# First tiles turned on TensorE, weights fetched ahead, and rows of tokens four tiles ahead, in a hybrid decoder step

## The chip, the core and the metric

The kernel runs on one core of one Trainium2 chip. The metric is the device time of one execution in microseconds (us), the median of several runs. The names of the engines: PE is TensorE (its weight loads are PEld), DVE is VectorE, ACT is ScalarE, POOL is GpSimd, SP is SyncE, which here issues all DMAs. An engine works through its instructions in a fixed order; where one of them waits, those behind it wait too.

## What is computed

One layer of a decoder with two kinds of mixers, for a prompt of 2048 tokens and for 64 sample tokens (8 sequences of 8). The rows x of 1024 numbers are normed, multiplied by one weight matrix of 3600 columns, and the columns are split up:

```python
def mixer_layer(x, pos, attend, s0, norm_w, w_in, ...):
    h = rmsnorm(x, norm_w)
    z = h @ w_in
    q, k, v, qb, kb, vb, g_lr, gate_a, gate_b = jnp.split(z, split_points(), axis=-1)
    q = rope(rmsnorm(heads(q, H_A), q_norm_w), pos)
    k = rope(rmsnorm(heads(k, H_A), k_norm_w), pos)
    o_a = attend(q, k, v)
    ...
    o_b, s_fin = gla_chunked(...)
    mixed = concatenate([o_a * silu(gate_a), rmsnorm(o_b) * silu(gate_b)])
    return x + mixed @ w_out, k, v, s_fin
```

`attend` is a mixture of three dilated windows over 8 heads of 64; `gla_chunked` is gated linear attention with 4 heads. Everything is in float32.

## The kernel before

**Products.** A product of float32 accuracy is made from float16 parts. A value is scaled and split into a high part (its float16) and a low part (the rest, as float16); three products (high by high, high by low, low by high) are summed in PSUM. For each row tile of 128 tokens and each block of weights (`v`, `q`, `k`, `qkb`, `g`, `vb`, `gb`, most with 512 columns) that is 8 slices of the contraction by 3 products, 24 matmuls at L1056. The 64 sample rows hold both parts in one stationary operand, 16 matmuls at L769.

**A row tile** (`prep`, L474): the row comes by DMA (`fetch`, L464), ACT squares and sums it (L487), `rsqrt` (L118) makes the scale with a few small steps on DVE and two on ACT, ACT writes the high part (L495), DVE the low part (L496). A DMA transpose turns both (L499) into `hl`, one of four buffers, the stationary operand; `hl` is also stored to DRAM for the later blocks (L503). The first four rows have two double buffers (tag `qq`) and a room of their own for the parts (`early_ht`); from tile 4 on there is one buffer for a row (tag `x`) and one for its parts (`ht`). The sample's rows are turned by PE (L510).

**A block of weights** (`load_w`, L544): eight DMAs bring 128x512 raw weights into eight buffers (tag `wr`). Then comes a size for the scale: for `v` the exact largest absolute value, by eight reductions on DVE (L566); for all other blocks a sum of squares, by eight steps on ACT (L572). `spread_max` (L533) takes the largest over the partitions by way of PE (L536, L539) and DVE (L538). From it a power of two follows, and then ACT writes the eight high parts (L603) and DVE the eight low parts (L604).

**The order of work.** First come `v`'s weights, the sample's rows and tiles 0 to 3 (L955 to L959). `first(0)` (L1076) then multiplies v for the sample and tiles 0 to 3, then q, then k. q's weights are loaded and split behind v's tile 0, k's behind v's tile 3; behind k of tile t, row t+4 is fetched and prepared. `first(1)` to `first(3)` go tile by tile through v, q, k, while units of attention (`attend`, L395: scores L408, mask and maximum on DVE L416, exponential on ACT L419, turning L426, values L441) are worked through in between; behind tile t, row t+4 is fetched and prepared, up to tile 15. Each block's result has a post: v is scaled and stored (L726, L734, L735); q and k are copied (`zs`, one buffer, L640 and L648), squared (L647), summed (L649), rotated on POOL (L672, L678) and scaled on DVE (L683, L684), split and stored (L756 to L760). Behind that follow the rest of the attention with `qkb`, the linear attention with `g`, `vb` and `gb`, and the output projection (L1422). Constants (`tabs`, `m3w`, `gnw`) are loaded by SP after the first tiles' code.

The order of the instructions on each engine, DMA issues on SP among them, is set by a scheduler that plays the program through in a timeline of its own (`schedule_with_timeline_sim=True`) and puts first what is ready first there; the order of the code is a preference only.

Of the kernel before, what the change touches and what calls it, by code (L numbers as in the profile page):

```python
# [7 lines left out]
F32 = mybir.dt.float32  # L8
# [44 lines left out]
def tile_hymba(ctx: ExitStack, tc: tile.TileContext, A: dict):  # L53
# [56 lines left out]
    for r0 in (0, 64):  # L110
        DVE.tensor_copy(ident64[r0 : r0 + 64], ident8[r0 : r0 + 64, r0 : r0 + 64])
    ones = cp.tile([P, 1], F32, name="ones")
# [234 lines left out]
    with ExitStack() as c1:  # L347
# [13 lines left out]
        wr = right(c_in, "wr", 8)  # L361
# [17 lines left out]
        again = [0]  # L379

# [83 lines left out]
        def fetch(t):  # L464
            n = NS if t == "s" else P
            if t in (0, 1, 2, 3):
                if t % 2 == 0:
                    early.append(ap_.tile([P, 2, D], F32, name=f"x_{t}", tag="qq"))
                x = xs[t] = early[-1][:, t % 2]
            else:  # L470
                x = xs[t] = xp.tile([P, D], F32, name=f"x_{t}", tag="x", bufs=1)
            SP.dma_start(x[:n], x_s if t == "s" else x_p[t * P : (t + 1) * P, :])

        def prep(t):  # L474
            again[0] += 1
            n = NS if t == "s" else P
            u = again[0]
            x = xs.pop(t)[:]
            if t == "s":
                hs = hps.tile([P, KT, 2 * NS], F16, name="hs")  # L480
                hi, lo = hs[:, :, 0:NS], hs[:, :, NS:]
            else:
                hl = hp.tile([P, 2, KT, n], F16, name=f"hl_{u}", tag="hl")
                hi, lo = hl[:, 0], hl[:, 1]
            ss = sm.tile([P, 1], F32, name=f"ss_{u}", tag="ss")
            jk = zp.tile([P, D], BF16, name=f"jk_{u}", tag="z1")
            ACT.activation(jk[:n], x[:n], AF.Square, accum_out=ss[:n])  # L487
            rs = sm.tile([P, 1], F32, name=f"rs_{u}", tag="rs")
            rsqrt(sm, rs[:n], ss[:n], 1.0 / D, n, 1, f"x{u}", H_SCALE)
            if t != "s":  # L490
                if t < 4:
                    ht = early_ht[:, t]
                else:
                    ht = xp.tile([P, 2, D], F16, name=f"ht_{u}", tag="ht", bufs=1)[:]
                ACT.activation(ht[:, 0], x, AF.Copy, scale=rs[:])  # L495
                DVE.scalar_tensor_tensor(  # L496
                    ht[:, 1], x, rs[:], ht[:, 0], ALU.mult, ALU.subtract
                )
                SP.dma_start_transpose(  # L499
                    hl[:].rearrange("p a k c -> p (a k) c"), ht.rearrange("p a c -> p (a c)")  # L500
                )
                hT[t] = (hi, lo)
                SP.dma_start(h_d[t * P : (t + 1) * P, :], hl[:].rearrange("p a k c -> p (a k c)"))  # L503
                return
            DVE.tensor_scalar(x[:n], x[:n], rs[:n], None, ALU.mult)
            for half in range(2):
                pt = ps_P.tile([P, 512], F32, name=f"ptx_{u}_{half}", tag="PT")
                for i in range(4):
                    k = 4 * half + i
                    PE.transpose(  # L510
                        pt[:, i * n : (i + 1) * n], x[:n, k * P : (k + 1) * P], ident[:n, :n]
                    )
                ptv = pt[:, : 4 * n].rearrange("p (k c) -> p k c", k=4)
                h = hi[:, 4 * half : 4 * half + 4, :]
                ACT.activation(h, ptv, AF.Copy)
                DVE.tensor_tensor(
                    lo[:, 4 * half : 4 * half + 4, :], ptv, h, ALU.subtract
                )
            hT[t] = hs
# [24 lines left out]
        def load_w(name, between=(), behind=()):  # L544

            if name in ("o0", "o1"):
                src, c0, n, rows, sh = w_out, 512 * int(name[1]), 512, None, 1.0
            else:
                src, (c0, n), rows, sh = w_in, BLOCKS[name], nw, H_SCALE
            raws = []  # L550
            mx = sm.tile([P, KT], F32, name=f"wm_{name}", tag="wm")
            for k in range(KT):
                raw = wr.tile([P, 528], F32, name=f"wr_{name}_{k}", tag="wr")
                SP.dma_start(raw[:, :n], src[k * P : (k + 1) * P, c0 : c0 + n])
                raws.append(raw)
# [3 lines left out]
            for f in behind:  # L559
                fetch(f)  # L560


            exact = name == "v"
            for k in range(KT):
                if exact:
                    DVE.tensor_reduce(  # L566
                        mx[:, k : k + 1], raws[k][:, :n], AX.X, ALU.max, apply_absolute_value=True
                    )
                else:
# [3 lines left out]
                        jk[:, :n], raws[k][:, :n], AF.Square, accum_out=mx[:, k : k + 1], **by  # L573
# [27 lines left out]
            for k in range(KT):  # L601
                h, l = w[:, 0, k, :n], w[:, 1, k, :n]
                ACT.activation(h, raws[k][:, :n], AF.Copy, scale=nws[:, k : k + 1])  # L603
                DVE.scalar_tensor_tensor(  # L604
                    l, raws[k][:, :n], nws[:, k : k + 1], h, ALU.mult, ALU.subtract
# [1216 lines left out]
```

## Time and profile before

| what | value |
|---|---|
| median of 3 runs | 1446.03 us (1445.89 to 1446.85) |
| the profiled execution's own time | 1444.89 us |
| its span in the profile | 1443.1 us |
| busy: PE, DVE, ACT, POOL | 89%, 70%, 59%, 43% of the span |
| mean granted PE clock | 0.961 |
| chain that ended last, by engine | PE 35%, DVE 22%, DMA 19%, ACT 10%, issue 8%, POOL 4% |
| DMA, mean | 198 GB/s |

The span runs from the first to the last instruction; all times in the views are counted from its start. The chain that ended last is followed back from the last instruction, at each step to what released it. "Issue" is time in which an engine waited for nothing that the profile shows. `a<-b` means that a is written from b, by the program's names, without buffer numbers. Below, "landing" is the time from a DMA's issue to its arrival.

### The profile page before, as it was taken

Reading aid. Unit: us, or ns where it says so; the run is one execution under the profiler, and the core shown is the slowest. Engines: PE = TensorE matmul, PEld = TensorE weight load, DVE = VectorE, ACT = ScalarE, POOL = GpSimd, SP = SyncE. Lnnn points to the kernel's source line nnn. Section 1 sums busy time; section 2 is a strip of 40 time slices with the busy share of each in tenths; the row PEclk is TensorE's granted clock in tenths of the full one; section 3 lists DMA queues with packets and bytes.
Section 4 is the critical chain, followed back from the end, with each engine's and each line's share of the span. In section 5 each row is a group of like instructions: output and inputs, shape, how many; then the busy total and the mean of one; then the engine's idle time right before and its main releaser. Section 6 shows DMA issues by size and latency. Waiting matters only on the chain.

```text
span 1443.1 us, 26500 instructions
## 1 busy us (share of the span) xinstructions
PE 1287.7 (89%) x8878; PEld 741.6 (51%) x8878; DVE 1013.1 (70%) x2445; ACT 853.1 (59%) x2295; POOL 624.8 (43%) x564
## 2 busy tenths in 40 slices
PE   4797998998989799997799999989889979999997
PEld 1343554555546455565466755667545435444343
DVE  6486877888798967667765446899978698773222
ACT  6635677677558866767667764778777543221120
POOL 0052334466667545664420376655752364340000
PEclk9998998999999999999799999999999999999998
DMA  9857585477866798879876453343225769988661
GB/s 280 253 163 181 149 215 145 125 204 224 207 181 190 171 271 260 281 231 245 233 186 161 137 169 103 101 133 119 71 103 192 258 203 339 377 286 267 227 205 62
DMA packets 255194, 285.36 MB, mean 198 GB/s; under 512 B 126209, under 2 KB 157010, under 8 KB 255058
## 3 DMA queue, kind: packets, MB, share of 16 engines
q1 hardware_dynamic: 255058, 283.67, 67.0%
q8 instruction: 70, 1.15, 0.3%
q14 instruction: 66, 0.54, 0.1%
HBM read 183.19 MB, written 75.24 MB: 179 GB/s over the span
## 4 chain that ended last, share of the span: by engine, by line
PE 35%; DVE 22%; DMA 19%; ACT 10%; issue 8%; POOL 4%; SPq 2%; DVEq 0%; POOLq 0%; ACTq 0%
PE Y L1422 8%; DMA T_q<-qp_d 3%; PE acc_vb L1056 3%; PE acc_g L1056 3%; PE OS L1671 3%; DMA x<-in_x_prompt 2%; PE s L408 2%; PE acc_q L1056 2%; PE acc_qkb L1056 2%; DVE p L416 2%; PE acc_v L1056 2%; DVE qbd L221 2%; PE t L426 2%; PE acc_k L1056 2%; ACT p L419 2%
## 5 line engine op out<-in xcount | busy, mean ns | idle before, releaser
L925 POOL TENSOR_TENSOR pr<-k,qb 128x512 f32<-128x512 f32 x128 | 174.8, 1366 | 188.7 <-DVE sck L926 111.7
L1056 PEld LDWEIGHTS <-hr 128*128 128x128 f16 x1824 | 177.6, 100 | 137.7 <-issue 16.5
L419 ACT ACTIVATE p<-p,o 128x256 f32<-128x256 f32 (+1 forms) x384 | 173.2, 453 | 84.3 <-DVE o L416 72.5
L1056 PEld LDWEIGHTS <-hl 128*128 128x128 f16 x1248 | 124.9, 102 | 157.5 <-issue 39.4
L1422 PE MATMUL Y<-w_o,mh 128*128 128x512 f16 x768 | 183.6, 387 | 10.4 <-ACT mh L1388 6.0
L416 DVE CUSTOM_DVE_ANT_0 p<-s,m3w,scl_s 128x256 f32<-128x256 f32 (+1 forms) x384 | 143.4, 418 | 34.4 <-DMA o_d<-o 20.8
L393 POOL TENSOR_TENSOR pt<-p,pt 128x512 f16<-128x512 f32 (+1 forms) x80 | 92.9, 1162 | 139.6 <-ACT pt L392 90.5
L441 PE MATMUL O<-v,pt 128*128 128x128 f16 x1200 | 115.6, 223 | 27.0 <-POOL pt L393 11.4
L426 PE MATMUL t<-ident,p 128*128 128x128 f32 x600 | 117.8, 286 | 14.3 <-ACT p L419 13.2
L1422 PEld LDWEIGHTS <-mh 128*128 128x128 f16 x768 | 72.8, 99 | 106.2 <-issue 27.1
L926 DVE TENSOR_REDUCE sck<-pr 128x8 f32<-128x512 f32 x128 | 87.1, 680 | 56.3 <-POOL pr L925 55.8
L408 PE MATMUL s<-kk,qq 128*128 128x256 f16 (+1 forms) x512 | 107.6, 324 | 17.5 <-DVE o L416 12.6
L1056 PE MATMUL acc_v<-w_v,hl 128*128 128x512 f16 x384 | 101.1, 410 | 13.0 <-ACT zs_k L648 4.6
L441 PEld LDWEIGHTS <-pt 128*128 128x128 f16 x1200 | 85.6, 100 | 51.8 <-POOL pt L393 15.7
L1056 PE MATMUL acc_g<-w_g,hr 128*128 128x272 f16 (+1 forms) x768 | 105.6, 288 | 5.3 <-DVE za L775 3.9
L1056 PE MATMUL acc_q<-w_q,hl 128*128 128x512 f16 x384 | 96.2, 394 | 2.1 <-ACT zs_q L648 1.4
L1056 PE MATMUL acc_k<-w_k,hl 128*128 128x512 f16 x384 | 92.9, 385 | 2.7 <-ACT zs_k L648 2.7
L1388 ACT ACTIVATE mh<-tm 128x1024 f16<-128x1024 f16 x32 | 31.7, 1020 | 104.1 <-PE tm L1387 97.7
L1056 PE MATMUL acc_vb<-w_vb,hr 128*128 128x512 f16 x384 | 91.4, 381 | 1.9 <-DVE so_g L622 1.9
L426 PEld LDWEIGHTS t<-ident,p 128*128 128x128 f32 x600 | 72.0, 145 | 36.0 <-ACT p L419 23.7
L1056 PE MATMUL acc_gb<-w_gb,hr 128*128 128x512 f16 x384 | 88.6, 384 | 0.1
L210 ACT ACTIVATE E<-D_e 128x256 f32<-128x256 f32 (+1 forms) x168 | 67.6, 412 | 31.7 <-DVE ks L217 21.2
(527 smaller groups left out, 2640.2 us busy)
## 6 DMA issues: line engine op xcount, KB each, us to landing
k<-in_cache_k_win SPq DMA_DIRECT2D x104, 256.0 KB, 4.4
sv<-in_cache_v_win SPq DMA_DIRECT2D x104, 256.0 KB, 5.5
hr<-h_d SPq DMA_DIRECT2D x44, 512.0 KB, 4.5
qb<-q_d SPq DMA_DIRECT2D x64, 256.0 KB, 4.7
oc<-o_d SPq DMA_DIRECT2D x48, 264.0 KB, 5.7
o_d<-o SPq DMA_DIRECT2D x64, 132.0 KB, 3.4
x<-in_x_prompt SPq DMA_DIRECT2D x16, 512.0 KB, 5.2
h_d<-hl SPq DMA_DIRECT2D x16, 512.0 KB, 5.1
```

The lines of the kernel that those rows point to most:

```text
L210: ACT.activation(E[rows, i, :n], D[rows, half], AF.Exp, scale=1.0 / 16.0)
L393: POOL.tensor_tensor(l, f, h, ALU.subtract)
L408: PE.matmul(s_ps[:, i * w : (i + 1) * w], q, k, start=(n == 0), stop=(n == len(prods) - 1),)
L416: DVE.tensor_tensor_reduce(s[:, sl], s_ps[:, sl], mask, neg, BIG, ALU.add, ALU.min, nmf(i))
L419: ACT.activation(s[:, sl], s[:, sl], AF.Exp, bias=nmf(i), scale=-1.0, accum_out=denf(i))
L426: PE.transpose(p_ps[:, i * P : (i + 1) * P], t["s"][:, i * P : (i + 1) * P], ident[:])
L441: PE.matmul(o_, t["pt"][:, c, (i * nb + b) * P : (i * nb + b + 1) * P], vf(i, b), start=(n == 0), stop=(n == 2 * nb - 1),)
L925: POOL.tensor_tensor(pr[:], kt, qt, ALU.mult)
L926: DVE.tensor_reduce(out, pr[:].rearrange("p (u k d) -> p u k d", u=2, k=4), AX.X, ALU.add)
L1056: PE.matmul(z, a_[:, k, :], w[:, p_, k, cols], start=(k == 0 and i == 0), stop=(k == KT - 1 and i == 2),)
L1422: PE.matmul(Y[:], a_[:, k, :], w_[:, part, k, :512], start=(i == 0), stop=(i == len(prods) - 1),)
L1671: PE.matmul(OS[32 * x : 32 * x + 32, 0:256], ps(x), vs_[bb][:, 256 * u : 256 * u + 256], start=(i == 0), stop=(i == 13),)
```

## The change

It touches the beginning of the kernel, up to the last prepared tile:

- Tiles 0 to 3 are turned by PE (64 transposes of 128x128 float16 with a float16 identity) into PSUM; ACT copies out the high parts, DVE the low parts. From tile 4 on, the DMA transpose stays.
- The order of ACT's instructions in this part is written out (`manual_schedule`): squares of the sample and tile 0, then tile 1's squares ahead of tile 0's scaling, the sample's copies, tile 0's copy, one `rsqrt` for tiles 1 to 3 together, then the split of v's weights, then tiles 1 to 3.
- `fetch_w` is taken out of `load_w`. q's raw weights are fetched right behind the first rows into buffers of the attention (`s`, `pt`) and of the cached keys (`k3`), k's as soon as v's raw buffers are free. For q and k the size is now the exact maximum too, on DVE; their DVE steps are queued behind a named DVE instruction (`issue_after`), the last low part before them. k's weights are split behind v's tile 2 instead of tile 3.
- The eight raw buffers become four pairs, and rows from tile 4 on use the same four buffers. Rows 4 to 7 are fetched behind k's weights, row t+8 behind the preparation of tile t+4.
- `zs` has two buffers.

The diff, cut to its core (in `prep`, `load_w` and the loops only what moves):

```diff
-        wr = right(c_in, "wr", 8)
+        wr = right(c_in, "wr", 4)
...
-                x = xs[t] = xp.tile([P, D], F32, name=f"x_{t}", tag="x", bufs=1)
+                pool, tag, bufs = (zp, "z3", 1) if t == "s" else (wr, "wr", 4)
+                x = pool.tile([P, 2, 512 if t == "s" else 528], F32, name=f"x_{t}", tag=tag, bufs=bufs)
+                x = xs[t] = x[:].rearrange("p a c -> p (a c)")[:, :D]
...
+        def prep_first(w_v):
...
+            def turned(t, a):
+                pt = (ps_S, ps_O)[a].tile([P, KT, P], F16, name=f"th_{t}_{a}", tag="SO"[a])
+                for k in range(KT):
+                    PE.transpose(
+                        pt[:, k, :], early_ht[:, t, a, k * P : (k + 1) * P], ident16[:]
+                    )
+                if a:
+                    last_low[0] = DVE.tensor_copy(hls[t][:, a], pt[:])
+                else:
+                    ACT.activation(hls[t][:, a], pt[:], AF.Copy)
+
+            squares("s", ss[:NS, 0:1])
+            rsqrt(xp, rs[:NS, 0:1], ss[:NS, 0:1], 1.0 / D, NS, 1, "xs")
+            squares(0, ss[:, 1:2])
+            rsqrt(xp, rs[:, 1:2], ss[:, 1:2], 1.0 / D, P, 1, "x0", H_SCALE)
+            for _ in range(KT):
+                next(w_v)
+            squares(1, ss[:, 2:3])
+            parts_of_rows(xs.pop(0), rs[:, 1:2], early_ht[:, 0])
...
+            squares(2, ss[:, 3:4])
+            next(w_v)
...
+            squares(3, ss[:, 4:5])
+            for a in range(2):
+                turned(0, a)
+            rsqrt(xp, rs[:, 2:], ss[:, 2:], 1.0 / D, P, 3, "x3", H_SCALE)
+            at_once(w_v)
+            for t in (1, 2, 3):
+                parts_of_rows(xs.pop(t), rs[:, t + 1 : t + 2], early_ht[:, t])
+            for t in (1, 2, 3):
+                for a in range(2):
+                    turned(t, a)
...
-            exact = name == "v"
+            exact = name in "vqk"
...
-                zs = xp.tile([P, 2, 512], F32, name=f"zs_{nm_}_{t}", tag="zs", bufs=1)
+                zs = xp.tile([P, 2, 512], F32, name=f"zs_{nm_}_{t}", tag="zs", bufs=2)
...
         fetch("s")
-        at_once(load_w("v", [0], [1, 2, 3]))
-        prep("s")
-        for t in range(4):
-            prep(t)
+        fetch_w("v", [0])
+        for t in (1, 2, 3):
+            fetch(t)
+
+        def q_place(k):
+
+            pool, tag = ((sp, "s"), (ptp, "pt"), (sk, "k3"))[k // 3]
+            return pool.tile([P, 512], F32, name=f"wr_q_{k}", tag=tag)[:]
+
+        fetch_w("q", places=q_place)
+        with tc.manual_schedule(engines={mybir.EngineType.Activation}):
+            prep_first(load_w("v"))
+        fetch_w("k")
...
                             if t == 0:
-                                at_once(load_w("q"))
-                            elif t == 3:
-                                at_once(load_w("k"))
+                                with tc.issue_after(last_low[0].ins):
+                                    at_once(load_w("q"))
+                            elif t == 2:
+                                with tc.issue_after(last_low[0].ins):
+                                    at_once(load_w("k"))
+                                for f in range(4, 8):
+                                    fetch(f)
                         elif name == "k":
-                            fetch(t + 4)
                             prep(t + 4)
+                            fetch(t + 8)
...
                 if t < 12:
-                    fetch(t + 4)
                     prep(t + 4)
+                if t < 8:
+                    fetch(t + 8)
```

More of the change, by code (lines that the diff above doesn't have):

```diff
@@ L111, in tile_hymba @@
         DVE.tensor_copy(ident64[r0 : r0 + 64], ident8[r0 : r0 + 64, r0 : r0 + 64])
+    ident16 = cp.tile([P, P], F16, name="ident16")
+    DVE.tensor_copy(ident16[:], ident[:])
     ones = cp.tile([P, 1], F32, name="ones")
@@ L558, in load_w @@
                         fetch(f)
-            for f in behind:
-                fetch(f)
-            exact = name == "v"
+        def load_w(name):
+            if name in ("o0", "o1"):
+                n, rows, sh = 512, None, 1.0
+            else:
+                n, rows, sh = BLOCKS[name][1], nw, H_SCALE
+            if name not in fetched:
+                fetch_w(name)
+            raws = fetched.pop(name)
+            mx = sm.tile([P, KT], F32, name=f"wm_{name}", tag="wm")
+            exact = name in "vqk"
             for k in range(KT):
@@ L602, in load_w @@
                 h, l = w[:, 0, k, :n], w[:, 1, k, :n]
-                ACT.activation(h, raws[k][:, :n], AF.Copy, scale=nws[:, k : k + 1])
-                DVE.scalar_tensor_tensor(
-                    l, raws[k][:, :n], nws[:, k : k + 1], h, ALU.mult, ALU.subtract
+                ACT.activation(h, raws[k], AF.Copy, scale=nws[:, k : k + 1])
+                last_low[0] = DVE.scalar_tensor_tensor(
+                    l, raws[k], nws[:, k : k + 1], h, ALU.mult, ALU.subtract
                 )
@@ L1369, in scales @@
             )
-        ident16 = cb1.tile([P, P], F16, name="ident16")
-        DVE.tensor_copy(ident16[:], ident[:])
         def parts_of(tag, mix):
```

102 lines of the change are left out of this document (52 added, 50 removed).

## Prediction, made before the result was known

> **What bounds the kernel now.** I read the page first. PE is busy 89% of the span, so most of the time PE is the limit, and a change to the beginning can only win where PE stands idle or runs slowly. So I asked next for busy times by stretches of the beginning. The columns are the stretch, its length, then busy time (and instruction count) of PE, its weight loads, DVE, ACT and POOL, then the granted PE clock, the DMA share and GB/s.
>
> ```profile
> PE 1287.7 (89%) x8878; PEld 741.6 (51%) x8878; DVE 1013.1 (70%) x2445; ACT 853.1 (59%) x2295; POOL 624.8 (43%) x564
> ```
> ```profile
> 25.00:62.00 37.00, 27.29 (x110) 11.46 (x111) 14.14 (x32) 24.70 (x55) 0.00 (x0) 0.95 0.94 277
> 62.00:107.00 45.00, 43.25 (x192) 19.09 (x191) 36.69 (x66) 21.02 (x45) 20.33 (x24) 0.96 0.62 176
> ...
> 119.00:160.00 41.00, 33.98 (x191) 18.02 (x189) 29.15 (x67) 24.69 (x69) 12.17 (x11) 0.88 0.62 158
> 160.00:205.00 45.00, 43.42 (x286) 25.64 (x284) 35.27 (x100) 34.26 (x107) 17.02 (x14) 1.00 0.71 197
> 25.00:119.00 94.00, 78.37 (x328) 33.63 (x329) 59.74 (x114) 50.37 (x109) 24.39 (x28) 0.93 0.76 213
> ```
>
> To 160 us PE has idle time and its clock is below 1; from 160 to 205 there is hardly either. PE's own order of time shows where (start, length, line, operation, and in brackets the idle time before it and what ended it).
>
> ```profile
> 25.17 4.31 PE L1056 MATMUL acc_v<-w_v,hl 128*128 128x512 f16 x13 [1.94 <-DMA hl<-early_ht]
> ...
> 37.47 6.18 PE L1056 MATMUL acc_v<-w_v,hl 128*128 128x512 f16 x20 [1.17 <-DMA hl<-early_ht]
> ...
> 52.20 5.34 PE L1056 MATMUL acc_v<-w_v,hl 128*128 128x512 f16 x24 [2.10 <-DVE vp L735]
> 60.56 0.27 PE L536 MATMUL mx_k<-ident,w_k 128*1 128x128 f32 x1 [3.02 <-DVE w_k L579]
> 61.20 0.38 PE L539 MATMUL mx_k<-mm_k,one_row 1*128 1x1 f32 x2 [0.37 <-DVE mm_k L538]
> 61.80 7.03 PE L1056 MATMUL acc_q<-w_q,hl 128*128 128x512 f16 x24 [0.22 <-DVE vp L735]
> 70.18 15.70 PE L1056 MATMUL acc_q<-w_q,hl 128*128 128x512 f16 x72 [1.35 <-ACT zs_q L648]
> 85.72 20.88 PE L1056 MATMUL acc_k<-w_k,hl 128*128 128x512 f16 x96
> 111.17 7.82 PE L1056 MATMUL acc_v<-w_v,hl 128*128 128x512 f16 x23 [4.56 <-ACT zs_k L648]
> 118.82 0.61 PE L408 MATMUL s<-kk,qq 128*128 128x128 f16 x8
> ```
>
> The undisturbed price of a 512-column product is 20.88/96 = 0.2175 us. After each pause the products are dearer: 7.82 for 23 where 5.0 is due, 7.03 for 24 where 5.2 is due. So a gap costs itself and 1.8 to 2.8 us of slow products behind it. The gaps have three owners: turned tiles that come by DMA (25.17, 37.47); the weights of q and k (60.56: k's maxima delay q, because they stand ahead of q in PE's order); and ACT, which is late with zs_k at 111.17 because it stood waiting for a row of tokens:
>
> ```profile
> 108.81 1.06 ACT L487 ACTIVATE jk<-x 128x1024 bf16<-128x1024 f32 x1 [5.57 <-DMA x<-in_x_prompt]
> ```
> ```profile
> ACT jk L487 <- DMA x<-in_x_prompt: 9.9, 5, 3.8
> ```
>
> The second is from ACT's waits between 119 and 215: 9.9 us for such rows, in five waits. The change aims at all three owners.
>
> **The change part by part.** The sum is made against the profiled execution: 1444.89 us, its span 1443.1, so 1.8 outside the span; the median of the runs is 1446.03, 1.1 above it.
>
> *Tiles 0 to 3 turned by PE.* Rows from PE's last stage, the view of the tile tm, and DVE's groups of 25 to 119 (busy us, mean ns, idle time before them):
>
> ```profile
> 1157.65 1.06 PE L1387 MATMUL tm<-ident,mt 128*128 128x128 f16 x16
> ```
> ```profile
> L1388 ACT ACTIVATE mh<-tm x32: 1005/1024/1026, 1163.7 to 1407.3; 128x1024 f16<-128x1024 f16 x32
> ```
> ```profile
> L496 DVE SCALAR_TENSOR_TENSOR early_ht<-x,rs,early_ht 128x1024 f16<-128x1024 f32 x3 | 3.8, 1278 | 1.2 <-ACT early_ht L495 1.2
> ...
> L735 DVE SCALAR_TENSOR_TENSOR vp<-acc_v,vp 128x512 f16<-128x512 f32 x4 | 2.7, 683 | 0.9 <-ACT vp L734 0.9
> ```
>
> Out go four DMA transposes on SP's queue, and with them the waits of 1.94 and 1.17. In come 64 turnings, 16 to a tile: 1.06 a tile by the first row. In come four copies out of PSUM on ACT (1.02 each) and four on DVE. For DVE's copy no row exists; the nearest are ACT's 1.02 for the same shape and twice the 0.68 that DVE needs for half of it from float32: 1.0 to 1.4, I take 1.2 (it is the same engine), 4.8 in all.
>
> *ACT's written order.* ACT's and DVE's order of time:
>
> ```profile
> 16.76 1.05 ACT L487 ACTIVATE jk<-x 128x1024 bf16<-128x1024 f32 x1
> ...
> 17.99 5.00 ACT L603 ACTIVATE w_v<-wr_v,ns_v 128x512 f16<-128x512 f32 x8
> ...
> 22.22 2.92 DVE L604 SCALAR_TENSOR_TENSOR w_v<-wr_v,ns_v,w_v 128x512 f16<-128x512 f32 x4
> ```
>
> The split of v's weights now stands behind tile 0's copy out of PSUM: 1.02 later, so its low parts end at 26.2 instead of 22.22+2.92 = 25.1. ACT also reads tile 1's squares before it scales tile 0, so a late row would hold everything behind it. The last of the four squares began at 16.76 before, ahead of the weights as well; I give this nothing, at worst 2. At 26.2 PE still has at least the five products of the last slice to do (1.1 us), at most all 40 of the sample and tile 0 (8.7): v's first part ends between 27.3 and 34.9, I take the middle, 31. Tiles 1 to 3 are 72 x 0.2175 = 15.7 and three turnings 3.2, so v ends at 49.9; before it was 52.20+5.34 = 57.5.
>
> *The weights of q and k ahead.* DVE's groups before 25, and DVE's order of time:
>
> ```profile
> L566 DVE TENSOR_REDUCE wm_v<-wr_v 128x1 f32<-128x512 f32 x8 | 5.4, 680 | 3.2 <-DMA wr_v<-in_w_in 3.1
> ```
> ```profile
> 60.35 0.16 DVE L579 TENSOR_REDUCE w_k<-wm_k 128x1 f32<-128x8 f32 x1 [8.20 <-ACT jw_k L572]
> ...
> 63.78 5.39 DVE L604 SCALAR_TENSOR_TENSOR w_k<-wr_k,ns_k,w_k 128x512 f16<-128x512 f32 x8 [0.79 <-ACT w_k L603]
> ```
>
> q's eight loads go out behind the first rows of tokens, into buffers that the attention (first product at 118.82) and the cached keys own. On SP the small constants stand behind them; the first of these on the path serves q's post, after 50 us. k's loads wait for v's raw buffers, free at 26, and are not read before 49. The maxima of both move from ACT to DVE (5.4 each). DVE's path to q's weights: 26.2 + 3.8 (low parts of three tiles) + 3.6 (their copies) + 1.4 (two v posts) + 5.4 (maxima) + 3.4 (60.35 to 63.78, from the maxima to the first low part) + 5.4 = 49.2. That is just ready as v ends, so q runs from 49.9 to 70.8 without a pause. k's: 49.2 + 5.4 + 3.4 + 5.4 = 63.4, and the posts of up to three q tiles in between. DVE did 36.7 between 62 and 107, less 5.4 for k's low parts, in about six posts and one prepared tile: at most 5.2 each, so k's weights are ready between 63 and 79. q ends at 70.8; I take the middle from there to the worst, 74.9, since DVE's order may put them first or last. Then k ends at 95.8 (91.0 at best, with v's first part early; at worst 79 + 20.9 + 2.8 for a pause = 102.7); before it was 85.72+20.88 = 106.6. That is **10.8**. If the cover of q's path is gone, each us of DVE delay costs one.
>
> *Rows four tiles ahead, zs in two buffers.*
>
> ```profile
> 92.26 1.06 ACT L487 ACTIVATE jk<-x 128x1024 bf16<-128x1024 f32 x1
> ...
> 104.28 0.32 SPq L503 DMA_DIRECT2D h_d<-hl  x1
> ```
>
> Rows 4 to 7 take the buffers that k's raw weights leave, between 63 and 79. From tile 4's squares to its turned tile took 12.0 (the two rows), so it is there between 80 and 96 when v asks at 95.8: just covered. ACT no longer stands before 108.8, so the idle **4.6** goes, and the slow products behind it, **2.8**. That is 18.2 by the end of tile 4's v. From 119 to 205 PE idles 7.0 and 1.6, and the clock of 0.88 over 41 us costs 4.9: 13.5 to be had. ACT's waits for rows there are 9.9; what is late next is the chain of an attention unit (PE, DVE, ACT in turn), which stays. Between 0 and 13.5 I take **6**, near the middle.
>
> *qkb's weights later.*
>
> ```profile
> L554 SPq DMA_DIRECT2D wr_qkb<-in_w_in x8: 327/328/359, 64.6 to 69.2; - x8
> L572 ACT ACTIVATE jw_qkb<-wr_qkb,nw x8: 715/721/737, 447.4 to 457.8; 128x512 bf16<-128x512 f32 x8
> ```
>
> Their raw buffers now hold rows until tile 15 is prepared, so the loads move from 65 us to some hundred us later. They are first read at 447, and issuing them took 5: nothing. Raw tiles freed in pairs come free one split (0.7) later, for weights that wait long anyway: nothing. After 205 the same work comes in a shifted order: 0, give or take 4.
>
> Sum: 10.8 + 4.6 + 2.8 + 6 = 24.2 less than 1444.9 is 1420.7, and with the median's 1.1 **1422**. With the good ends (15.6, 7.4, 13.5) it is 1410, with the poor ones (3.9, 4.6, 0) 1438.
>
> **A rule that speaks against it.** The 16 turnings in 1.06 us followed full-speed products. The Trainium skill (TensorE: Matmul & The Clock Gate, Part 4: PE-mode transpose) says that transposes don't count as busy for the gate that raises PE's clock. No run here shows that; by the rule the third rival below is what happens.
>
> **The rivals.** *DVE becomes the bound, with a smaller gain.* DVE was busy 59.74 from 25 to 119; 10.8 of maxima and 4.8 of copies make 75.3. My forecast needs all of it but some 8 (the last posts) between 26 and 101: a share of 0.90. At the share of 62 to 107, 36.69/45 = 0.82, the stage ends at 26 + 92 = 118, no earlier than now, and only the 6 behind it are won: 1440. For it: the posts are long where POOL works too. Against: the maxima fill time in which DVE had little (14.14 of 37).
>
> *The same, on the other side.* If the maxima are waited for one after the other and DVE stays at its share of 59.74/94 = 0.64, 75.3 takes 118 us and the stage ends at 144, 25 late: 1446 + 25 - 6 = 1465. From a share of 75.3/94 = 0.80 downwards this decides. Against: what DVE waited for (8.20 before 60.35: maxima on ACT behind late loads) is gone.
>
> *The turnings leave PE slow.* Each of three tiles' turnings between v's products is followed by slow products, 2.8 as after 111.17: 8.4 dearer, 1430.
>
> *The rows still come late*, so that the change doesn't do what it says: the 6 are lost, 1428, inside the forecast. *All waits go*: 1410. *Later stages give it back* by their shifted order: 1446.
>
> **How the numbers follow.** Executions can differ by about 0.2%, 2.9 us; less can't be told from no change. Chances: forecast (1415 to 1434) 0.60; DVE bound with a smaller gain 0.17, 0.01 of it within the 2.9; slow turnings 0.07; all waits gone 0.05; given back 0.04; slower 0.07. So faster 0.88, same 0.05, slower 0.07. From 1409 to 1440 lie the forecast, the slow turnings and most of the small and the large gain: 0.82.
>
> **What would show it.** Right: acc_v of tile 3 ends near 50, acc_q follows without a pause, acc_k ends near 96, acc_v of tile 4 starts with it at 0.22 a product, and ACT waits for no row of tokens from 60 on. Wrong in size: a gap ahead of acc_k released by DVE w_k, with DVE above 90%. Wrong in sign: DVE below 0.80 up to the first attention product, and that product after 119. If the beginning wins 18 and the total doesn't, the loss lies behind 205.

## The result, and the profile after

The changed kernel takes **1425.88 us** (median of 4 runs, 1424.45 to 1427.22), the kernel before 1446.44 beside it. The ratio over all runs is 0.9847, with a 95% interval from 0.9817 to 0.9877: 1.5% faster; the medians differ by 20.6 us. The prediction said 1422 (1409 to 1440), with faster as the likely case. The profiled execution took 1426.68 us, its span 1424.9. The total is within the range, 3.9 above the forecast, and by another way than the one worked out, as the stages show.

From the page of the changed kernel, the busy time of each engine:

```profile
PE 1285.0 (90%) x8942; PEld 743.6 (52%) x8942; DVE 1018.0 (71%) x2459; ACT 843.7 (59%) x2259; POOL 621.9 (44%) x564
```

PE has 64 instructions more (the turnings) and yet 2.7 us less busy time, in a span that is 18.2 shorter: what was removed is idle time (15.5) and slow products. Where, is in the busy times by stretches, with the columns as before:

```profile
25.00:62.00 37.00, 34.19 (x188) 16.40 (x187) 27.19 (x60) 18.93 (x28) 2.29 (x3) 1.00 0.60 209
62.00:107.00 45.00, 39.62 (x173) 17.16 (x172) 41.13 (x89) 26.26 (x57) 20.02 (x24) 0.94 0.63 180
...
119.00:160.00 41.00, 38.45 (x250) 22.89 (x249) 32.97 (x76) 28.70 (x81) 18.43 (x15) 1.00 0.81 207
160.00:205.00 45.00, 42.84 (x283) 24.75 (x282) 34.14 (x94) 34.14 (x108) 20.18 (x15) 1.00 0.67 187
25.00:119.00 94.00, 85.81 (x418) 39.09 (x417) 76.92 (x172) 52.22 (x104) 26.00 (x31) 0.96 0.68 206
```

From 25 to 62 PE is busy 34.19 us where it was 27.29. From 62 to 107 it is *less* busy than before (39.62 against 43.25), and DVE stands at 41.13/45 = 0.91. From 119 to 160 the clock is 1.00 where it was 0.88, and 250 instructions fit in where there were 191. PE's order of time says what happened:

```profile
30.66 1.95 PE L512 MATMUL th<-ident,early_ht 128*128 128x128 f16 x32
...
35.29 5.34 PE L1120 MATMUL acc_v<-w_v,hl 128*128 128x512 f16 x24
...
50.94 1.68 PE L1120 MATMUL acc_v<-w_v,hl 128*128 128x512 f16 x7
...
53.51 5.23 PE L1120 MATMUL acc_q<-w_q,hl 128*128 128x512 f16 x23 [0.41 <-DVE w_q L659]
...
69.15 0.27 PE L577 MATMUL mx_k<-ident,w_k 128*1 128x128 f32 x1
69.26 4.70 PE L1120 MATMUL acc_q<-w_q,hl 128*128 128x512 f16 x21
73.89 0.38 PE L580 MATMUL mx_k<-mm_k,one_row 1*128 1x1 f32 x2
...
77.60 0.38 PE L1120 MATMUL acc_k<-w_k,hl 128*128 128x512 f16 x1 [1.28 <-ACT w_k L658]
78.38 20.78 PE L1120 MATMUL acc_k<-w_k,hl 128*128 128x512 f16 x95 [0.41 <-DVE w_k L659]
102.85 8.15 PE L1120 MATMUL acc_v<-w_v,hl 128*128 128x512 f16 x24 [3.69 <-DMA hl<-ht]
...
112.99 0.61 PE L408 MATMUL s<-kk,qq 128*128 128x128 f16 x8
```

v ends at 52.6 (before 57.5), k at 99.2 (before 106.6). But v of tile 4 does not join on: PE waits 3.69 us, now for the turned tile, and its 24 products again take 8.15, where 5.2 is due. By the end of that block (111.0, before 119.65) the gain is 8.6 us. Most of the rest appears in the stage from 119 to 205, where the attention is interleaved.

Why the turned tile is late stands in three orders of time, SP's, ACT's and DVE's:

```profile
80.90 2.42 SPq L474 DMA_DIRECT2D x<-in_x_prompt  x4
98.45 2.11 SPq L496 DMA_TRANSPOSE hl<-ht  x1
```
```profile
76.82 5.01 ACT L658 ACTIVATE w_k<-wr_k,ns_k 128x512 f16<-128x512 f32 x8 [2.89 <-DVE ns_k L649]
...
86.54 1.05 ACT L481 ACTIVATE jk<-x 128x1024 bf16<-128x1024 f32 x1
...
93.13 1.14 ACT L484 ACTIVATE ht<-x,rs 128x1024 f16<-128x1024 f32 x1
```
```profile
52.70 5.39 DVE L659 SCALAR_TENSOR_TENSOR w_q<-wr_q,ns_q,w_q 128x512 f16<-128x512 f32 x8 [0.79 <-ACT w_q L658]
...
77.58 5.39 DVE L659 SCALAR_TENSOR_TENSOR w_k<-wr_k,ns_k,w_k 128x512 f16<-128x512 f32 x8 [0.20 <-ACT w_k L658]
```

Rows 4 to 7 can only be fetched as k's split has read its raw weights, pair by pair, from 80.9; DVE reads the last of them until 83.0. From tile 4's squares (86.54) to its turned tile (102.8) it takes 16.3 us; before it was 12.0. ACT waits for no row of tokens after 60: that line is gone from its waits.

### The profile page after: what moved, and what is told of

It is laid out like the page before. It is cut to its first block, busy times and chain, and to the rows that moved or that the text cites. A ratio compares the mean times of both kernels' runs of the same rounds, so it can differ in the third digit from the quotient of the medians.

```text
span 1424.9 us, 26506 instructions
## 1 busy us (share of the span) xinstructions
PE 1285.0 (90%) x8942; PEld 743.6 (52%) x8942; DVE 1018.0 (71%) x2459; ACT 843.7 (59%) x2259; POOL 621.9 (44%) x564
## 4 chain that ended last, share of the span: by engine, by line
PE 35%; DVE 25%; DMA 16%; ACT 11%; issue 7%; POOL 4%; SPq 2%; DVEq 0%; POOLq 0%; ACTq 0%
PE Y L1488 7%; PE acc_g L1120 3%; PE acc_vb L1120 3%; PE acc_k L1120 3%; DMA k<-in_cache_k_win 2%; POOL pr L980 2%; PE s L408 2%; PE OS L1737 2%; PE acc_qkb L1120 2%; ACT p L419 2%; DMA o_d<-o 2%; DMA oc<-o_d 2%; DVE p L416 2%; PE acc_v L1120 2%; DMA T_q<-qp_d 2%
## 5 line engine op out<-in xcount | busy, mean ns | idle before, releaser
L980 POOL TENSOR_TENSOR pr<-k,qb 128x512 f32<-128x512 f32 x128 | 171.8, 1342 | 184.9 <-DVE sck L981 113.9
L393 POOL TENSOR_TENSOR pt<-p,pt 128x512 f16<-128x512 f32 (+1 forms) x80 | 98.3, 1229 | 139.6 <-ACT pt L392 107.3
L1488 PEld LDWEIGHTS <-mh 128*128 128x128 f16 x768 | 72.5, 99 | 103.7 <-issue 25.2
L1120 PE MATMUL acc_q<-w_q,hl 128*128 128x512 f16 x384 | 92.0, 380 | 1.9 <-ACT zs_q L703 1.4
```

The source lines that it names most:

```text
L393: POOL.tensor_tensor(l, f, h, ALU.subtract)
L980: POOL.tensor_tensor(pr[:], kt, qt, ALU.mult)
L1120: PE.matmul(z, a_[:, k, :], w[:, p_, k, cols], start=(k == 0 and i == 0), stop=(k == KT - 1 and i == 2),)
L1488: PE.matmul(Y[:], a_[:, k, :], w_[:, part, k, :512], start=(i == 0), stop=(i == len(prods) - 1),)
```

## The experiments

The question was which part carries the 20 us, given that the visible gain at 111 is only 8.6. The theory: PE's turnings and the early weights win the beginning, and the rows fetched four tiles ahead win the stage behind it. The rivals: the second `zs` buffer is what frees PE there; DVE is the bound in the beginning; the later stages move by themselves, whatever is edited.

For all kernels, in us: the start of v's tile 4; the start of the last product of k in the profile's view of that tile, which closes the stage with prepared rows; the time from there to the end of the span, in code that no edit touches; and the median, with its ratio to the kernel before. The first three come from the one profiled execution, the last two from all runs. The ratio is taken to runs of the kernel before on the same chip, whose median was 1447.5 beside e1 to e4, 1448.9 beside e5 to e8 and 1449.1 beside e9 to e12.

| kernel | v of tile 4 | last product of k | from there to the end | median | ratio, 95% interval |
|---|---|---|---|---|---|
| before | 111.2 | 470.8 | 972.3 | 1446.4 | |
| changed | 102.9 | 451.8 | 973.1 | 1425.9 | 0.9847 [0.9817, 0.9877] |
| e1, rows one ahead, one `zs` | 103.7 | 470.7 | 986.7 | 1459.2 | 1.0077 [1.0052, 1.0102] |
| e2, one `zs` | 99.0 | 447.1 | 980.0 | 1426.2 | 0.9838 [0.9806, 0.9871] |
| e3, tiles turned by DMA | 108.8 | 470.9 | 965.1 | 1440.3 | 0.9946 [0.9929, 0.9962] |
| e4, weights fetched behind | 102.4 | 452.9 | 977.7 | 1432.5 | 0.9889 [0.9863, 0.9915] |
| e5, before with rows four ahead | 114.2 | 461.5 | 979.1 | 1440.8 | 0.9958 [0.9937, 0.9978] |
| e6, size on ACT | 98.6 | 450.9 | 981.6 | 1433.5 | 0.9893 [0.9858, 0.9927] |
| e7, tile 4 earlier | 97.2 | 454.5 | 974.0 | 1431.6 | 0.9900 [0.9867, 0.9934] |
| e8, ACT's order free | 101.3 | 449.1 | 974.4 | 1429.1 | 0.9864 [0.9829, 0.9900] |
| e9, changed with an idle step | 100.2 | 448.8 | 979.2 | 1427.0 | 0.9839 [0.9809, 0.9869] |
| e10, changed with an idle step | 102.5 | 453.7 | 975.9 | 1429.5 | 0.9858 [0.9830, 0.9886] |
| e11, before with an idle step | 110.7 | 474.2 | 969.8 | 1447.2 | 0.9990 [0.9969, 1.0010] |
| e12, before with an idle step | 109.6 | 473.2 | 975.1 | 1445.9 | 0.9981 [0.9961, 1.0001] |

**e1: rows one tile ahead, `zs` in one buffer,** the rest of the change kept.

```diff
-                pool, tag, bufs = (zp, "z3", 1) if t == "s" else (wr, "wr", 4)
...
+                    x = xs[t] = xp.tile([P, D], F32, name=f"x_{t}", tag="x", bufs=1)[:]
...
-                zs = xp.tile([P, 2, 512], ..., tag="zs", bufs=2)
+                zs = xp.tile([P, 2, 512], ..., tag="zs", bufs=1)
...
-                                for f in range(4, 8):
-                                    fetch(f)
...
+                            fetch(t + 4)
                             prep(t + 4)
-                            fetch(t + 8)
```

> The changed kernel with its rows from tile 4 on fetched as before: one buffer of their own, each row one tile ahead, and zs in one buffer (there is no room for two beside it). Theory A (the gain of some 10 us between tile 4's v and 212 us comes from the rows): these 10 are lost, 1436 us give or take 4, and ACT again waits 6 to 10 us for rows between 110 and 215. Theory B (it comes from zs's second buffer): 1436 too, but then the next run, which takes away the second buffer alone, shows the same time. Theory C (neither: PE merely runs on at full clock after a better beginning): 1426 give or take 3.

Measured: 1459.2, slower than the kernel before and than any of the three theories allowed. The beginning is as good as in the changed kernel (103.7), but behind it the gain is lost. ACT's waits between 60 and 215, and the stretch from 119 to 160:

```profile
ACT jk L483 <- DMA x<-in_x_prompt: 16.8, 5, 5.8
```
```profile
119.00:160.00 41.00, 31.98 (x174) 16.89 (x173) 25.02 (x48) 21.06 (x53) 11.74 (x11) 0.83 0.60 158
```

The waits for rows are back (15.4 us in this stretch in the kernel before), PE is busy 31.98 us where the changed kernel has 38.45, and its clock falls to 0.83. At k's last product the gain is gone (470.7). So without rows in time, the rest of the change wins nothing by then. Another 8 to 14 us are lost behind it (986.7, where the changed kernel and its repeats below have 973.1 to 979.2), and no row is fetched there; their cause was not isolated.

**e2: `zs` in one buffer,** nothing else (the second pair of lines above).

> The changed kernel with one buffer for zs, all else kept. Theory A (rows): 1426 to 1428, no more than 2 us from the changed kernel. Theory B (zs): 1434 to 1438, with PE or ACT waiting for zs between 110 and 215.

Measured: 1426.2. The second buffer is worth nothing that can be seen, so what e1 lost belongs to the rows.

**e3: the tiles turned by DMA again,** all else as changed (ACT's written order with the copies left out; DVE's steps for q queue behind the last low part of a row, for there is no copy to name).

```diff
-                pt = (ps_S, ps_O)[a].tile([P, KT, P], F16, ...)
-                for k in range(KT):
-                    PE.transpose(...)
...
+                    SP.dma_start_transpose(
+                        hls[t][:].rearrange("p a k c -> p (a k) c"),
+                        early_ht[:, t].rearrange("p a c -> p (a c)"),
+                    )
```

> The changed kernel with tiles 0 to 3 turned by DMA transposes as before, everything else kept. Theory A (the turning by PE is worth what the tiles would come later): tile 1 comes by about 37 to 39 instead of 33, so v's end moves from 52.6 to 55 to 58, and 1429 to 1432 in all. Rival: q's weights are ready at 52.7 only, and v has slack up to there, so the turning by PE is worth nothing: 1424 to 1427.

Measured: 1440.3, dearer than expected. PE's order of time:

```profile
27.78 4.06 PE L1118 MATMUL acc_v<-w_v,hl 128*128 128x512 f16 x18 [1.38 <-DMA hl<-early_ht]
...
36.03 6.18 PE L1118 MATMUL acc_v<-w_v,hl 128*128 128x512 f16 x20 [2.68 <-DVE tabs L1053]
...
52.86 7.03 PE L1118 MATMUL acc_v<-w_v,hl 128*128 128x512 f16 x24 [4.08 <-DVE vp L788]
63.59 6.52 PE L1118 MATMUL acc_q<-w_q,hl 128*128 128x512 f16 x22 [3.71 <-DVE vp L788]
```

The waits of 1.38 and 2.68 are both for a turned tile: the second is put down to a step of DVE, but the weight load of the same product stood until the tile landed (first row below). Then v's posts come late (4.08 and 3.71), each with slow products behind it. They are late by way of ACT, which stood 13.15 us until the sample's v was stored (second row):

```profile
36.03 0.11 PEld L1118 LDWEIGHTS <-hl 128*128 128x128 f16 x2 [3.17 <-DMA hl<-early_ht]
```
```profile
50.25 0.69 ACT L779 ACTIVATE vs<-acc_v,wi_v 128x512 f32<-128x512 f32 x1 [13.15 <-DMA v_d<-vs_s]
```

On SP's queue that store was issued at 44.92, behind three turnings (29.79 to 38.38), the stores of turned rows and loads of k's weights; in the changed kernel it was issued at 36.05. v ends at 59.9 instead of 52.6. So the turning by PE carries much of the beginning, 7.3 us at v's end and 14 in the total, and the trace points to SP's queue as the place where the turnings by DMA cost most.

**e4: the weights of q and k fetched where they are split,** not ahead, q's too into the raw buffers.

```diff
-        fetch_w("q", places=q_place)
...
-        fetch_w("k")
```

> The changed kernel with the raw weights of q and k fetched where they are split, as before, in the four pairs; sizes still on DVE. Theory A: q's loads come at about 28 to 35, in time for its sizes at 36, so q loses nothing; k's loads can go only once q's split has freed the buffers, 58 to 66 instead of 25 to 33, so k's weights are 7 to 9 us later than 77.6 and PE waits ahead of k: 1432 to 1436. Rival (DVE bounds k's weights in any case): under 3 us, 1426 to 1429.

Measured: 1432.5. The total is what fetching ahead would explain, the trace is not. q's loads go out later, but its maxima on DVE start no later (34.3 against 36.1). The rows of the tile `wr_q`, first in the changed kernel, then in e4:

```profile
L601 SPq DMA_DIRECT2D wr_q<-in_w_in x8: 327/328/328, 10.6 to 17.2; - x8
L621 DVE TENSOR_REDUCE wm_q<-wr_q x8: 676/678/679, 36.1 to 40.2; 128x1 f32<-128x512 f32 x8
```
```profile
L601 SPq DMA_DIRECT2D wr_q<-in_w_in x8: 327/375/424, 22.0 to 26.3; - x8
L621 DVE TENSOR_REDUCE wm_q<-wr_q x8: 676/677/678, 34.3 to 38.5; 128x1 f32<-128x512 f32 x8
```

k's loads go out at 52.3 instead of 24.9, and its weights are not the 7 to 9 us later that were expected: its first product comes at 76.9 (77.6 in the changed kernel). v's tile 4 starts at 102.4, as in the changed kernel. The early fetch itself wins nothing in the beginning. Most of the loss in the profiled pair comes behind k's last product. One stage there, between 800 and 840 us, looks much worse in e4; the rows are those of the changed kernel, of e10 and of e4:

```profile
800.00:840.00 40.00, 38.77 (x245) 23.91 (x244) 17.20 (x42) 21.61 (x61) 28.02 (x39) 1.00 0.54 156
```
```profile
800.00:840.00 40.00, 39.15 (x247) 23.99 (x245) 18.29 (x45) 21.61 (x62) 28.40 (x41) 1.00 0.55 153
```
```profile
800.00:840.00 40.00, 36.17 (x222) 22.16 (x222) 14.22 (x52) 22.61 (x73) 18.64 (x32) 0.91 0.50 145
```

e10 has PE's, ACT's, POOL's and SP's instructions in the very order of the changed kernel and repeats their busy times to 0.4 us, DVE's to 1.1. In e4 the order on SP and DVE differs from early on, on PE and ACT from some 700 us on (but for one product). PE waits there, is busy 2.6 us less, and the clock drops to 0.91. But from 900 to 1100 PE is busy 2.9 us more than in the changed kernel (181.44 against 178.57), and the 977.7 from k's last product to the end lie within the 973.1 to 979.2 of the changed kernel and its repeats. So no stage is shown that holds e4's loss.

**e5: the kernel before with rows four tiles ahead alone** (pairs of raw buffers, `fetch` as in the change).

```diff
-                x = xs[t] = xp.tile([P, D], F32, name=f"x_{t}", tag="x", bufs=1)
+                pool, tag, bufs = (zp, "z3", 1) if t == "s" else (wr, "wr", 4)
...
+                                for f in range(4, 8):
+                                    fetch(f)
...
-                            fetch(t + 4)
                             prep(t + 4)
+                            fetch(t + 8)
```

> The kernel before with one part of the change alone: raw buffers in four pairs, and rows from tile 4 on in them, four tiles ahead. Theory A (ACT's 5.6 us before 109 and 9.9 us between 119 and 215, spent waiting for rows, are the loss): the waits for rows vanish, the last product of k (470.8 us before, 451.8 in the changed kernel) comes 10 to 18 us earlier, 1430 to 1436 in all. Theory D (rows ahead pay only on top of the better beginning, since e1 with a late row each was slower than the kernel before): last product of k within 5 us of 470.8, 1441 to 1449.

Measured: 1440.8, some 6 to 8 us faster than before; k's last product comes 9.3 us earlier (461.5). That is less than theory A and more than theory D asked for. PE's order of time at v's tile 4, and the stretch behind it:

```profile
114.21 6.64 PE L1059 MATMUL acc_v<-w_v,hl 128*128 128x512 f16 x24 [6.00 <-DMA hl<-ht]
```
```profile
119.00:160.00 41.00, 39.52 (x252) 22.77 (x251) 30.77 (x74) 30.45 (x81) 15.47 (x14) 1.00 1.07 269
```

The waits of ACT for rows are gone and the clock is 1.00 from 119 to 160, as in the changed kernel. At the same time row 4 comes later than before, for it waits for k's raw buffers: 6.00 us. So rows four ahead have a price in the beginning, which the faster beginning lowers (3.69 in the changed kernel) but does not take away.

**e6: the size of q and k from sums of squares on ACT** again.

```diff
-            exact = name in "vqk"
+            exact = name == "v"
```

> The changed kernel with the sizes of q's and k's weights as sums of squares on ACT, as before; everything else kept. That takes some 10 us of work from DVE between 36 and 63 us and gives ACT some 14. Theory A (PE's order decides: k's first product follows the second step of the maximum, which stands behind 21 products of q): k's first product within 3 us of 77.6, 1424 to 1430. Rival (DVE is the bound of the beginning, as in the prediction's first rival): k's first product comes 4 us or more earlier and 1418 to 1422.

Measured: 1433.5. DVE gets 4 us freer between 25 and 119 (72.65 instead of 76.92), ACT 11 us busier (63.50 instead of 52.22). k's first product comes at 75.2, and v's tile 4 starts 4 us earlier than in the changed kernel, 1.6 earlier than in e9, a repeat of it:

```profile
98.64 7.03 PE L1120 MATMUL acc_v<-w_v,hl 128*128 128x512 f16 x24 [2.56 <-ACT zs_k L703]
```

It doesn't help the total. So DVE as the bound of the beginning is not borne out; since ACT got the work that DVE lost, what DVE alone costs there is not shown.

**e7: row 4 fetched and split into parts during q,** with other room for two of k's raw tiles, so that v's tile 4 need not wait. Tiles 5 to 7 are split one step earlier too.

```diff
+            if k >= 6:
+                return sk.tile([P, 512], ..., tag=("pr", "k2")[k - 6], bufs=1)[:]
...
+        fetch(4)
...
+                        elif name == "q" and t == 3:
+                            prep_parts(4)
+                            fetch(8)
```

> The changed kernel with tile 4 prepared earlier: two of k's raw weights lie in buffers of the cached keys' dots, so that row 4 has a raw pair from 28 us on; tile 4's parts are made behind q's tile 3 instead of behind k's tile 0, and only the DMA transpose waits for tile 0's buffer; tiles 5 to 7 likewise one step earlier. Theory A (v of tile 4 waits 3.7 us for its turned tile and then pays slow products): the wait goes, tile 4's v starts within 1 us of k's end and ends 5 to 7 us earlier than 111.0, and of that at least half is left at the end, 1419 to 1423. Rival (the later stages eat it): 1424 to 1430.

Measured: 1431.6. The wait is gone:

```profile
97.19 4.92 PE L1140 MATMUL acc_v<-w_v,hl 128*128 128x512 f16 x22
...
111.80 0.86 PE L426 MATMUL t<-ident,p 128*128 128x128 f32 x2 [2.91 <-ACT p L419]
...
114.37 4.43 PE L1140 MATMUL acc_k<-w_k,hl 128*128 128x512 f16 x10 [0.32 <-DVE vp L799]
```

v's tile 4 starts 5.7 us earlier than in the changed kernel and at full speed, and at k's last product nothing is left of it (454.5). Removing the gap that the prediction had overlooked wins nothing. The trace shows where it goes at first: behind tile 4's q, PE stands 2.91 us for the exponential of an attention unit, and ten products then take 4.43 us, 2.1 more than at full speed. In the changed kernel PE waits for nothing between tile 4's q and k. That the attention's chain paces the stage behind is suggested by this and not isolated, for e7 changes the room of k's weights and the order of three more tiles as well.

**e8: ACT's order left to the scheduler.**

```diff
-        with tc.manual_schedule(engines={mybir.EngineType.Activation}):
-            prep_first(load_w("v"))
+        prep_first(load_w("v"))
```

> The changed kernel without the written order of ACT in the beginning; the scheduler orders it. Theory A (the written order only guards a sequence that the scheduler would nearly find): first product of v within 2 us of 21.4, 1424 to 1430. Rival (the order is worth its place: the split of v's weights would otherwise mix with the scaling of tiles 1 to 3): v's weights split 3 to 5 us later, 1430 to 1434.

Measured: 1429.1, and the interval overlaps that of the changed kernel for the larger part. The difference of 3.2 us is no larger than between repeats of one order (below): what the written order is worth cannot be told from nothing.

**e9 to e12: one idle step more on DVE,** in the changed kernel and in the kernel before, to see how far times move by themselves.

```diff
+            DVE.tensor_copy(idle[:], ident[:, 0:8]) if m == 0 else None
```

> The changed kernel with one idle step more on DVE (a copy of 128x8 float32 into a tile that nobody reads, some 0.1 to 0.2 us), written behind first(0); nothing is left out. Theory E: the time behind the stages that were edited depends on the scheduler's order, which any edit ahead of it reshuffles; then this kernel differs from the changed one (1425.9) by 3 to 12 us in either direction, and the time from the last product of k to the end, 974.9 there, lies elsewhere between 967 and 989, though no edit touches that code. Rival: the order behind is stable, and the later losses seen in the other runs (989.4 with rows one tile ahead, 979.6 with the weights behind) were caused by their edits; then this kernel takes 1425 to 1428 and that remainder 974 to 976.

> The changed kernel with the same idle DVE step written behind first(1); nothing is left out. Theory E: the beginning up to the second pass is as in the changed kernel (v's tile 4 starts within 1 us of 102.9), and the total differs by 3 to 12 us in either direction. Rival: 1425 to 1428, with a remainder behind k's last product of 974 to 976.

> The kernel before with the idle DVE step written behind first(0); nothing is left out. Theory E: the total differs from the kernel before by 3 to 12 us in either direction, so that single differences of this size between kernels of this study are no evidence for a part of the change. Rival: within 2 us of the kernel before.

> The kernel before with the idle DVE step written behind first(1); nothing is left out. Theory E: v's tile 4 starts within 1 us of 111.2, and the total differs from the kernel before by 3 to 12 us in either direction. Rival: within 2 us of the kernel before.

Measured: 1427.0 and 1429.5 beside the changed kernel's 1425.9; 1447.2 and 1445.9 beside 1446.4. The theory as put (3 to 12 us from any edit) is not borne out: three of the four differ by 1.1 us or less, e10 by 3.6. But the step was placed elsewhere than it was written; the view of its tile in e9:

```profile
L1178 DVE COPY idle<-ident x1: 165/165/165, 2.9 to 2.9; 128x8 f32<-128x8 f32 x1
```

It depends only on a constant, so the scheduler put it at 2.9 us, and the other instructions of all five engines kept their order. The four kernels therefore do not test what another order costs. They are repeats of the same order, and better than that test: they show what doesn't count. With an unchanged order the remainder behind k's last product lay between 973 and 979 in the changed kernel (three executions), between 970 and 975 in the kernel before, and the medians of the changed order within 3.6 us of each other; all its 16 runs lie between 1421.0 and 1431.8, those of the kernel before, taken beside all these, between 1440.1 and 1457.0. By that measure e2 and e8 equal the changed kernel. e4, e6 and e7 are 4.6 to 6.5 us slower than the middle of the three medians (1427.0), but their intervals overlap that of e10: likely, not shown. e1, e3 and e5 are beyond doubt.

## Why the prediction was right, and where its steps failed

- **v's end (forecast 49.9): right, short by one term.** Measured 52.6, and in the two repeats of the order (e9, e10) 50.5 and 50.9. ACT, whose order is written out, stood 1.9 to 2.0 us for row 1 in all three, the cost that the prediction put at "nothing, at worst 2"; in the changed kernel's own profile row 1 also landed 1.1 us later than in the repeats.
- **q without a pause: nearly right, and by another way.** q ran from 52.7 to 76.3 with gaps of 0.41 and 1.35 us, where 49.9 to 70.8 was forecast. The forecast let q start when its weights are wholly split, at 49.2. Measured, the last low part was done at 58.1 (52.70 + 5.39), 8.9 later; it cost little because PE started on the first parts while the others were still being split. That q followed on v so closely is in part luck: the late split and the overlap that the sum left out made up for each other.
- **k's end (95.8): off by 3.4.** Measured 99.2. k's first product came at 77.6 instead of 74.9, and its last low part at 83.0, outside the "63 to 79" that the prediction gave for k's weights. PE was with q until 76.3, 5.5 later than forecast, and stood 1.7 for k's weights. A part of that wait comes from PE's own queue: the second step of k's maximum stood behind 21 products of q, from 69.26 to 73.96, while DVE had its part done at 70.45. The prediction had seen the reverse in the profile before (k's maxima ahead of q in PE's order) and costed neither in its own plan. It explains 1.7 us at most; the rest is the later end of q. So 7.4 instead of 10.8.
- **"Rows 4 to 7 take the buffers that k's raw weights leave, between 63 and 79 … just covered": this step failed.** Two terms were too small. k's split ended at 83.0, 4 behind the worst of the forecast, so that row 4 was fetched at 80.9. And from its squares to the turned tile it took 16.3 us instead of the 12.0 taken over from the profile before: 3.2 more on ACT and DVE, where posts of q and k stand between the squares and the low part (done at 96.2), and 1.3 more on SP, where the DMA transpose came behind others (issued at 98.45). So the tile was there at 102.8, where "between 80 and 96" was forecast. The idle 4.6 became 3.7, and 3 us of slow products stayed. Of the 18.2 by the end of tile 4's v, 8.6 came (some 10 in the mean of three executions of each order).
- **"A gap costs itself and 1.8 to 2.8 us of slow products": too general.** In the prediction's own rows two pauses have no slow products behind them: 24 in 5.34 us behind 2.10 (52.20), 72 in 15.70 behind 1.35 (70.18). In e9, the same order as the changed kernel, the pause before tile 4's v was nearly the same and its products ran at full speed:

```profile
100.18 5.35 PE L1120 MATMUL acc_v<-w_v,hl 128*128 128x512 f16 x24 [3.17 <-DMA hl<-ht]
```

In e6 they took 7.03 behind 2.56. The length of the pause alone does not decide it; what does, the runs do not show.
- **The stage behind (6, of 13.5): under-sized.** From 119 to 205 PE idles 4.7 instead of 8.6, and the clock of 1.00 saves the whole 4.9, together 8.8. With the 8.6 before it that is 17.4 by 205.
- **"0, give or take 4" after 205: right.** The gain is 19.0 at k's last product (470.8 against 451.8) and 18.2 at the end of the spans (1443.1 against 1424.9). In the mean of the three executions of each order (e9 to e12 with the first two) it is 21.3 there (472.7 against 451.4), and 3.7 are given back behind it (972.4 against 976.1).
- **DVE as the bound: rightly kept as a rival.** Its share from 62 to 107 was 0.91, over the 25 to 119 of the sum 0.82, and yet the first product of the attention came at 113.0 instead of 118.8, where the rival had it come no earlier. Its copies out of PSUM took less than assumed, by the groups from 25 to 119:

```profile
L516 DVE COPY hl<-th 128x1024 f16<-128x1024 f16 x3 | 2.1, 684 | 0.9 <-PE th L512 0.9
```

0.68 each instead of 1.2. The Trainium skill (VectorE: DVE Perf Modes, Why PSUM operands drop a tier) says that an operand in PSUM allows at most a doubled rate, and only the single rate for float32. The same 0.68 for twice the elements of the float32 row from which the 1.2 was scaled agrees with that.
- **Slow turnings: not so here.** The 24 products at 35.29, behind 16 turnings, took 5.34 us. A product alone shows 0.38, 0.16 above the pitch of 0.2175; (5.34 - 0.16)/24 is 0.216, full speed.
- **The sum:** 24.2 forecast, 18.2 in the profiled pair, 20.6 by the medians. The beginning was put 9.6 too high, the stage from 119 to 205 2.8 too low; the second error took back part of the first, and that the total came out 3.9 from the forecast is in part luck. The 2.9 us that the prediction allowed between executions was too little: the 16 runs of the changed order spread over 10.8. The rival "rows still late" priced late rows at 6 us. With them e1 loses 33 against the changed kernel, 18.9 of it by k's last product; e5 gains 6 to 8 on the kernel before by rows in time alone. Parts of this change don't add up: e1 lacks one part and is slower than the kernel without any.

What stays open: why e1 loses another 8 to 14 us behind k's last product, and e3 gains some 8 there (965.1 against 973.1). That another order of the instructions is the cause is not shown.

## What to carry to other kernels

A buffer that is to be reused early comes free at the *last read* of its old content: follow the chain to that read, and on to the product that waits, through every queue it crosses (here DVE's split, the posts on ACT and DVE, and SP's queue), before calling a fetch covered. Where a change of several parts is timed by taking parts out, look for parts that are worth something only together, and time repeats of one order first: in this kernel 3 us between two variants say nothing. And a wait that is removed counts only if no other wait takes its place: e7 removed 3.7 us of wait and 3 of slow products, met a new wait of 2.9 with slow products behind it, and won nothing.

## What the runs showed of the hardware

Turnings cost 1.03 us for 8 ahead of v's first products and 1.95 for 32 between full-speed products, 0.13 against 0.06 each. Behind the first ones PE was not at full speed, and those in between did not take it away. The rows of PE's order of time in the changed kernel:

```profile
16.87 1.03 PE L512 MATMUL th<-ident,early_ht 128*128 128x128 f16 x8 [0.85 <-ACT early_ht L484]
18.19 1.03 PE L512 MATMUL th<-ident,early_ht 128*128 128x128 f16 x8 [0.29 <-DVE early_ht L485]
21.42 0.58 PE L824 MATMUL acc_v_s<-w_v,hs 128*128 128x512 f16 x1 [2.20 <-ACT w_v L658]
21.80 0.63 PE L1120 MATMUL acc_v<-w_v,hl 128*128 128x512 f16 x1
22.23 1.06 PE L824 MATMUL acc_v_s<-w_v,hs 128*128 128x512 f16 x2
23.08 1.49 PE L1120 MATMUL acc_v<-w_v,hl 128*128 128x512 f16 x3
```

From 21.42 to 23.08 the products start 0.41 us apart (four in 1.66), half the later rate. The Trainium skill's rule that transposes don't count as busy for the clock (TensorE: Matmul & The Clock Gate, Part 4: PE-mode transpose) fits the first rows. They do not prove it, for PE also stood idle for 2.20 us just before its first product. For turnings among products the fear drawn from the rule was unfounded here, where at most 1.95 us of them stand together; longer runs of turnings were not tried.
